# A macaron block on one Trainium2 core: the first FFN's last product as seven half products, transposed back for the mixer

## The chip, the cores and the metric

The kernel runs on one core of a Trainium2 chip. The core has five engines that run side by side and meet through semaphores: TensorE (PE, matrix products into PSUM; PEld is its loading of the stationary operand), VectorE (DVE), ScalarE (ACT), GpSimd (POOL) and SyncE (SP, which here only issues DMAs). The metric is the device time of one execution in microseconds (us). Three executions of the kernel before took 1169.32, 1170.34 and 1170.53 us; the median is 1170.34.

## The reference, cut to what matters

One layer, 512 tokens of 1024 channels, all float32; the inner width of an FFN is 2816.

```python
x = x + 0.5 * swiglu(rms_norm(x, ffn1_norm), ffn1_w1, ffn1_w3, ffn1_w2)   # (silu(h@w1) * (h@w3)) @ w2
h = rms_norm(x, mix_norm)
p = h @ w_in                               # 1024 x 5384: RWKV-7 columns, FoX columns, gates
...                                        # RWKV-7 recurrence, forgetting attention, gates
x = x + (gate_a * y_a + gate_b * y_b) @ w_out
x = x + 0.5 * swiglu(rms_norm(x, ffn2_norm), ffn2_w1, ffn2_w3, ffn2_w2)
out = rms_norm(x, final_norm)
```

## The kernel before

The program works through five stages in turn: the first FFN (FFN1), the mixer's input products with its preparation, the recurrence and the attention, the mixer's output products, and the second FFN (FFN2). Channels lie on the 128 partitions and the 512 tokens along the free axis, so `x` is kept as eight tiles `xT[c]` of 128 x 512.

**Products.** To keep float32 accuracy each operand is split into a high part (rounded to the format in which TensorE takes 512 columns in one pass) and a low remainder, and a product of a 128 x 128 weight block with 128 x 512 data is three matmuls: high*high, high*low, low*high (`mm3`, lines 122 to 124). For a block of eight weight tiles ACT makes the high part `whi` (L114) and DVE the low part `wlo` (L115). `whi` and `wlo` have two buffers each, the loaded `raw` tiles three.

**FFN1 and FFN2 up to the hidden values.** `ffn` (L453) runs over 22 blocks `j` of the hidden width. For each, `pa` and `pb` collect 8 x 3 matmuls, then `hidden` scales them with the token's `rstd`, applies SiLU and multiplies.

**The last product of FFN1** takes the hidden values as they are. `hidden` splits each block into `hh{j}` and `hl{j}`. For each of the eight channel tiles `m`, `pd` collects 22 x 3 matmuls with w2 blocks that are loaded in three pieces of 8, 8 and 6; DVE adds half of it to `xT[m]` (L518), and `mix_add(m)` saves the tile to DRAM through POOL's queue (L525), makes the mixer's operands `xh`, `xl` from it, and squares it for the norm.

**The last product of FFN2** uses `Seven` (L1147): both the hidden width and the output channels (and the tokens) are cut in halves, and a Strassen-like scheme forms the 2 x 2 block product from seven half-size products, with sums and differences of the blocks as operands. The sums of the weight blocks are made by DMA: a load through POOL's queue with `accum_op=add` adds the next block onto a tile `sum[g]` already in SBUF (L1195), and plain loads go through SP (L1197). Each of the seven products has 11 steps `k` and two halves `i` of 128 tokens, three matmuls each: 66 matmuls of 128 x 512. Its six weight tiles ("slots", two steps each) lie in tiles that earlier work has left: slot 0 in two `raw` tiles, slots 1 and 2 in `xh`, `xl` tiles, slots 3 and 4 in `whi`/`wlo`, slot 5 in the third `raw` tile. Here the data is the stationary operand and the weights are the moving one, so a result has tokens on the partitions and is added to a tile `O` of tokens x channels. That suits the kernel's output, which is stored so.

**The seam between FFN1 and the mixer.** The mixer's first two units are `psa` (72 columns of w_in) and `psg` (96 columns), both named `pl`, in the two banks of the PSUM pool `pm`. Behind `psa` two matmuls `ssum` add up the squares over the channels; ACT makes `rstd` from them (`finish`, with a load of the logarithm's table, L127); four transposes `rct` turn `rstd` to tokens on partitions (`rc`). DVE multiplies each unit by `rstd` (`u`, L583). From `psa` come `codes`, which the eight products `pz` need; these stand inside the two units `pk` that follow.

**What sets the order.** The program is written as one stream; the framework's planner puts each engine's instructions into an order of its own by a model of their times, within the data's dependences and with hints (`tc.issue_after`). On the chip each engine and each DMA queue takes its instructions strictly in that order, so an instruction that waits holds those behind it.

## Time and profile before

| | us |
|---|---|
| median of three runs | 1170.34 (1169.32 to 1170.53) |
| the profiled execution's own time | 1169.42 |
| its span, from the first to the last instruction | 1167.6 |
| TensorE busy in the span | 1150.1 (98%) |
| VectorE busy | 691.4 (59%) |
| ScalarE busy | 497.1 (43%) |
| GpSimd busy | 110.2 (9%) |
| mean DMA rate | 112 GB/s |

All starts below are counted from the span's start. A row of the timeline has start, length, engine, line, operation, the tile that it writes and those that it reads. Matmuls overlap in the pipeline, so the time that one adds to a stream is the distance between starts, not its own length. In a row of the windows the numbers behind the stretch are its length and then the busy time of PE, PEld, DVE, ACT and POOL, each with its count, the granted TensorE clock (1.00 is full), the DMA engines' share and their GB/s.

### The profile page before, as it was taken

What the parts mean: (1) busy time and instruction counts of PE and PEld (TensorE: products, weight loads), DVE (VectorE), ACT (ScalarE), POOL (GpSimd) and SP (SyncE); (2) the same over time, 40 slices, a digit from 0 to 9 for tenths busy, and PEclk for the clock granted to TensorE, in tenths of its full rate; (3) what the DMA queues carried; (4) which work ended last, traced back from release to release, by engine and by line L of the source; (5) the groups of instructions that cost most, each with busy time, mean ns of one, the idle gap of its engine ahead of it and who ended that gap; (6) DMA issues with size and microseconds to landing.
All of it is one profiled execution on the core that took longest, in us unless ns stands there. A gap on an engine that the chain in (4) does not pass through costs nothing.

```text
span 1167.6 us, 15706 instructions
## 1 busy us (share of the span) xinstructions
PE 1150.1 (98%) x6190; PEld 933.5 (80%) x6190; DVE 691.4 (59%) x996; ACT 497.1 (43%) x790; POOL 110.2 (9%) x159
## 2 busy tenths in 40 slices
PE   9999999999999999999999999899999999999997
PEld 7888888888887888887777786678888888888886
DVE  6645545543444598776776765677343446367874
ACT  6322222222223755345877665533332223236654
POOL 1200000001111111321000011112000000003210
PEclk9999999999999999999999999999999999999999
DMA  6333333333333333345112235543333333329981
GB/s 181 113 108 91 91 109 90 92 98 117 117 112 102 97 107 111 113 139 136 37 37 90 82 103 158 181 126 109 109 108 90 93 105 91 98 66 182 234 196 73
DMA packets 197865, 131.19 MB, mean 112 GB/s; under 512 B 10238, under 2 KB 180286, under 8 KB 197790
## 3 DMA queue, kind: packets, MB, share of 16 engines
q1 hardware_dynamic: 185198, 104.74, 30.6%
q0 software_dynamic: 9776, 23.60, 8.8%
q10 hardware_dynamic: 2816, 1.84, 0.5%
q8 instruction: 49, 0.80, 0.3%
q14 instruction: 26, 0.21, 0.1%
HBM read 119.47 MB, written 10.68 MB: 111 GB/s over the span
## 4 chain that ended last, share of the span: by engine, by line
PE 93%; ACT 2%; DVE 2%; DMA 2%; issue 1%; SPq 0%; ACTq 0%; DVEq 0%
PE pb L124 7%; PE pb L122 7%; PE pb L123 7%; PE pa L124 7%; PE pa L122 7%; PE pa L123 7%; PE pd L123 3%; PE pd L124 3%; PE pd L122 3%; PE pgt L122 3%; PE pgt L124 2%; PE pgt L123 2%; PE pk L123 2%; PE pk L122 2%; PE pk L124 2%; PE X L124 1%
## 5 line engine op out<-in xcount | busy, mean ns | idle before, releaser
L114 ACT CAST whi<-raw 128x1024 fp32r<-128x1024 f32 (+2 forms) x174 | 173.6, 999 | 510.7 <-PE pa L123 158.4
L115 DVE TENSOR_TENSOR wlo<-raw,whi 128x1024 fp32r<-128x1024 f32 (+2 forms) x174 | 202.2, 1162 | 86.7 <-ACT whi L114 86.7
L124 PE MATMUL pb<-xh,wlo 128*128 128x512 f32 x344 | 134.8, 392 | 0.1
L123 PE MATMUL pb<-xl,whi 128*128 128x512 f32 x344 | 134.1, 390 | 0.0
L124 PE MATMUL pa<-xh,wlo 128*128 128x512 f32 x344 | 134.1, 390 | 0.0
L122 PE MATMUL pb<-xh,whi 128*128 128x512 f32 x344 | 134.0, 390 | 0.0
L122 PE MATMUL pa<-xh,whi 128*128 128x512 f32 x344 | 134.0, 389 | 0.0
L123 PE MATMUL pa<-xl,whi 128*128 128x512 f32 x344 | 134.0, 389 | 0.0
L466 DVE TENSOR_TENSOR fb<-pb,rstd 128x512 f32<-128x512 f32 x43 | 29.7, 691 | 132.3 <-PE pb L124 132.3
L462 DVE TENSOR_TENSOR fa<-pa,rstd 128x512 f32<-128x512 f32 x43 | 29.7, 691 | 82.1 <-PE pa L124 82.1
L124 PEld LDWEIGHTS pb<-xh,wlo 128*128 128x128 f32 x344 | 64.6, 188 | 13.7 <-DVE wlo L247 0.6
L123 PEld LDWEIGHTS pb<-xl,whi 128*128 128x128 f32 x344 | 64.6, 188 | 13.6
L123 PEld LDWEIGHTS pa<-xl,whi 128*128 128x128 f32 x344 | 64.6, 188 | 13.5
L124 PEld LDWEIGHTS pa<-xh,wlo 128*128 128x128 f32 x344 | 64.6, 188 | 13.4
L122 PEld LDWEIGHTS pa<-xh,whi 128*128 128x128 f32 x344 | 64.6, 188 | 13.3
L122 PEld LDWEIGHTS pb<-xh,whi 128*128 128x128 f32 x344 | 64.6, 188 | 13.1
L122 PE MATMUL pd<-hh,whi 128*128 128x512 f32 x176 | 68.5, 389 | 0.0
L123 PE MATMUL pd<-hl,whi 128*128 128x512 f32 x176 | 68.5, 389 | 0.0
L124 PE MATMUL pd<-hh,wlo 128*128 128x512 f32 x176 | 68.5, 389 | 0.0
L122 PE MATMUL pgt<-xh,whi 128*128 128x512 f32 x128 | 53.7, 419 | 0.0
L123 PE MATMUL pgt<-xl,whi 128*128 128x512 f32 x128 | 50.4, 393 | 0.0
L124 PE MATMUL pgt<-xh,wlo 128*128 128x512 f32 x128 | 50.2, 392 | 0.0
(482 smaller groups left out, 2231.9 us busy)
## 6 DMA issues: line engine op xcount, KB each, us to landing
raw<-in_ffn_w_dram SPq DMA_DIRECT2D x102, 512.0 KB
raw<-in_w_in_dram SPq DMA_DIRECT2D x40, 512.0 KB
raw<-in_w_out_dram SPq DMA_DIRECT2D x8, 512.0 KB
xS<-in_ffn_w_dram POOLq DMA_DIRECT2D x8, 512.0 KB, 8.1
raw<-in_ffn_w_dram SPq DMA_DIRECT2D x8, 384.0 KB
xS<-in_ffn_w_dram SPq DMA_DIRECT2D x6, 512.0 KB
gsave<-gs SPq DMA_DIRECT2D x9, 256.0 KB
xin<-in_x_dram SPq DMA_DIRECT2D x8, 256.0 KB
```

Source lines behind the costliest of these rows:

```text
L114: (hi_eng or act).copy(hi[:], raw[:])
L115: (eng or dve).tensor_tensor(lo[:], raw[:], hi[:].bitcast(F32), op=ALU.subtract)
L122: pe.matmul(ps, whi, xhi, start=first, stop=False, skip_group_check=onto)
L123: pe.matmul(ps, whi, xlo, start=False, stop=False, skip_group_check=onto)
L124: return pe.matmul(ps, wlo, xhi, start=False, stop=last, skip_group_check=onto)
L462: dve.tensor_tensor(a[:], pa[:], nrm.rstd[:], op=ALU.mult)
L466: dve.tensor_tensor(b[:], pb[:], nrm.rstd[:], op=ALU.mult)
```

## The change

FFN1's last product is done by `Seven` as well. The class moves ahead of FFN1 and gets two children: `Last` for FFN2 (as before), `Middle` for FFN1. `Middle` adds onto a tile `O1` of tokens x channels, into which x is loaded a second time during the hidden blocks, with the first weight sums. During the seventh product each 128 x 128 block of `O1` is turned back by a transpose on TensorE (`turn`, L672): channel tiles 4 to 7 first, copied to `xT` by ACT, saved, and scaled to `xh`, `xl`; of tiles 0 to 3 the token blocks 2 and 3 at once, 0 and 1 behind the last matmuls, all in four PSUM banks (`low`) from which the mixer's operands are made directly. The units `psa` and `psg` take channel tiles 4 to 7 first, then 0 to 3. The norm's sums of squares now come from `O1` (ACT, with an accumulating output, four per half of the channels); `root` makes `rc` from them on 128 x 4 values, and `spread_root` brings it to all partitions with one float32 matmul (`rows`) against four diagonal tiles `dg`. `ssum`, `rct`, the squares of `xT` and POOL's additions of them are gone at this place. Tiles 0 to 3 are copied to `xT` and saved later (`keep`). The two first `pk` units get banks of the pool `pf`.

In both FFNs the seventh product now takes its steps in the order 0, 1, 6 to 10 for both halves, then 2 to 5 for one half after the other (before: 0 to 5, then 6 to 10), the sixth product's two results are added in the other order, and two weight splits are placed a little earlier.

```diff
+    KH, TH, LO, HI = KF // 2, T // 2, slice(0, D // 2), slice(D // 2, D)
+    class Seven:
...
+        def load(s, n, g):
+            r, c, more = ((0, 0, 0), (0, 1, 1), (1, 1, 1), (1, 0, 1), (1, 1, 0), (0, 1, 1), (1, 0, 0))[n]
...
+            if more:
+                nc.gpsimd.dma_start(s.sum[g], src, accum_op=ALU.add)
+            else:
+                with tc.issue_after(loads[-1].ins):
+                    nc.sync.dma_start(s.sum[g], src)
...
+            for n in range(6):
+                for g in range(6):
+                    put(n, min(2 * g + (5 if n == 0 else 3), 11 if n == 5 else 99), s.weight, n + 1, g)
...
+            first_k, last_k = (0, 1, 6, 7, 8, 9, 10), (2, 3, 4, 5)
+            for k in first_k:
+                for i in range(2):
+                    s.mm = mm(V, 6, i, k, True)
+                for f, *a in after.get((6, k), ()):
+                    f(*a)
+                s.between(k)
+            for i in range(2):
+                for k in last_k:
+                    s.mm = mm(V, 6, i, k, True)
+                    s.ending(i, k)
+                s.out(V[i][:], i, LO, 0.5)
+                s.finished(i)
...
-    def mix_add(c):
-        nc.gpsimd.dma_start(xsave[c], xT[c][:])
-        mix.add(c)
-
-    ffn(nrm, ffn1_w1, ffn1_w3, ffn1_w2, mix_add, {2: load_params, 4: masks, 10: place_params}, (first, second))
+    class Middle(Seven):
+        def turn(s, c, bs, ps=None, behind=None):
+            if ps is None:
+                ps = bank("xt", pm)
+            with tc.issue_after(behind.ins):
+                for b in bs:
+                    s.turned = pe.transpose(ps[:, b * P:(b + 1) * P], s.O[:, b, c * P:(c + 1) * P], ident[:])
+            return ps
...
+        def between(s, k):
+            if k == 7:
+                s.low = [bank(f"xt{c}", q_) for c, q_ in enumerate((pf, pf, pr, pr))]
+            c = {7: 4, 8: 5, 9: 6, 10: 7}.get(k)
+            if c:
+                ps = s.turn(c, range(NB), behind=s.mm)
+                act.copy(xT[c][:], ps[:])
+                nc.gpsimd.dma_start(xsave[c], xT[c][:])
+                mix.scale(c)
+                s.turn(c - 4, (2, 3), s.low[c - 4], s.mm)
+
+        def ending(s, i, k):
+            if i == 1 and k == 3:
+                for c in range(4):
+                    s.turn(c, (0,), s.low[c], s.mm)
...
+    def tail(s, behind):
+        for c in range(4):
+            s.turn(c, (1,), s.low[c], behind)
+        for c in range(4):
+            s.parts = mix.scale(c, act, s.low[c][:])
+        with tc.issue_after(s.parts[0].ins):
+            s.power(1, LO, sums[0])
+
+    def root(rc):
+        dve.tensor_tensor(rc, sums[0][:], sums[1][:], op=ALU.add)
+        act.activation(rc, rc, AF.Ln, bias=epsr[:, 0:1], scale=1.0 / D)
+        act.activation(rc, rc, AF.Exp, scale=-0.5)
+        dg = tmp("dg")
+        for b in range(NB):
+            dve.tensor_scalar(dg[:, b * P:(b + 1) * P], ident[:], rc[:, b:b + 1], None, op0=ALU.mult)
+        return dg
+
+    def spread_root(dg, behind):
+        ps = bank("rows", pr)
+        with tc.issue_after(behind.ins):
+            pe.matmul(ps[:], ones, dg[:], start=True, stop=True)
+        mix.rstd = xp.tile([P, T], F32, tag="rstd", name="rstd")
+        dve.tensor_copy(mix.rstd[:], ps[:])
+
+    def keep(s):
+        for c in range(4):
+            act.copy(xT[c][:], s.low[c][:])
+            nc.gpsimd.dma_start(xsave[c], xT[c][:])
...
+    ffn(nrm, ffn1_w1, ffn1_w3, ffn1_w2, make1, {2: load_params, 4: masks, 10: place_params}, (first, second),
+        {5 + 2 * j: (lambda j=j: beside1(j)) for j in range(8)})
...
-        mms = mix.cols(psa[0:72, :], *load_w([(0, W[:, COL_W:COL_W + 64]), (64, W[:, COL_F:COL_F + 8])], KD, 72), 72)
-        mix.parts()
-        summed = mix.finish(mms[-1])
...
+        mms = mix.cols(psa[0:72, :], *wa, 72, [seven1.turned] * 2, ks=(4, 5), end=False)
+        tail(seven1, mms[-1])
+        mms = mix.cols(psa[0:72, :], *wa, 72, [seven1.turned] * 2, ks=(6, 7), begin=False, end=False)
+        mms = mix.cols(psg[0:96, :], *wg, 96, [mms[-1]] * 4, ks=range(4, KD), end=False)
+        mms = mix.cols(psa[0:72, :], *wa, 72, [mms[-1]] * 4, ks=range(4), begin=False)
+        mms = mix.cols(psg[0:96, :], *wg, 96, [mms[-1]] * 4, ks=range(4), begin=False)
+        with tc.issue_after(seven1.parts[0].ins), tc.issue_after(seven1.parts[1].ins):
+            diag = root(rc[:])
+        spread_root(diag, mms[1])
         tc.keep_in_program_order(act.preload_act_table_set("sigmoid_and_others"))
-        mix.cols(psg[0:96, :], *load_w(win(COL_G, 96), KD, 96), 96, [summed])
...
+        keep(seven1)
+        o1.close()
...
-            ps = bank("pk")
+            ps = bank("pk", pf)
```

In the order of TensorE's instructions, this stood at the seam from FFN1 to the mixer: the last six matmuls of `pd` and the first six of the unit `psa`, whose tile is named `pl`.

```order
L122 MATMUL pd<-hh_1884,whi 128x512
L123 MATMUL pd<-hl_1885,whi 128x512
L124 MATMUL pd<-hh_1884,wlo 128x512
L122 MATMUL pd<-hh_1958,whi 128x512
L123 MATMUL pd<-hl_1959,whi 128x512
L124 MATMUL pd<-hh_1958,wlo 128x512
L122 MATMUL pl<-xh_2049,whi 72x512
L123 MATMUL pl<-xl_2050,whi 72x512
L124 MATMUL pl<-xh_2049,wlo 72x512
L122 MATMUL pl<-xh_2049,whi 72x512
L123 MATMUL pl<-xl_2050,whi 72x512
L124 MATMUL pl<-xh_2049,wlo 72x512
```

Now TensorE has there, behind the last three matmuls of the seventh product (`V` is its PSUM tile), transposes into the four banks `xt` of tiles 0 to 3 and, between two groups of them, the first six matmuls of `psa`, on channel tiles 4 and 5.

```order
L123 MATMUL V_1933<-sxl_1894,q_354 128x512
L124 MATMUL V_1933<-sxh_1893,q_354 128x512
L672 MATMUL xt_2521<-ident,O_339 128x128
L672 MATMUL xt_2522<-ident,O_339 128x128
L672 MATMUL xt_2523<-ident,O_339 128x128
L672 MATMUL xt_2524<-ident,O_339 128x128
L122 MATMUL pl<-xh_2532,whi 72x512
L123 MATMUL pl<-xl_2533,whi 72x512
L124 MATMUL pl<-xh_2532,wlo 72x512
L122 MATMUL pl<-xh_2532,whi 72x512
L123 MATMUL pl<-xl_2533,whi 72x512
L124 MATMUL pl<-xh_2532,wlo 72x512
```

Four more transposes stand behind these rows, then 18 matmuls on tiles 4 to 7, 24 on tiles 0 to 3, `rows`, and the first `pk` unit; from the second `pk` unit on, the order of TensorE is that of before, but for the places of single `pz` and `pn` matmuls.

ScalarE's rows at the same place, before: the last squares and the norm, with two table loads and the cast `whi` for the first `pk` unit between them.

```order
L187 ACTIVATE sq<-xT_115 128x512
L202 CAST shi<-acc 128x512
L127 ACT_TABLE_LOAD
L114 CAST whi<-raw 128x1024
L129 ACTIVATE rln<-ssum,epsr 128x512
L213 ACTIVATE rstd<-rln 128x512
L570 ACT_TABLE_LOAD
L561 ACTIVATE la<-u,omu 64x512
```

Now: the operands of tiles 0 to 3, the last square, the four copies of `keep`, `root`, a table load, and only then the casts for the two `pk` units.

```order
L175 ACTIVATE xh_2685<-xt_2523,par 128x512
L175 ACTIVATE xh_2685<-xt_2524,par 128x512
L592 ACTIVATE osq,ss_341<-O_339 128x512
L729 COPY xT_108<-xt_2521 128x512
L729 COPY xT_108<-xt_2522 128x512
L729 COPY xT_109<-xt_2523 128x512
L729 COPY xT_109<-xt_2524 128x512
L713 ACTIVATE rc<-rc,epsr 128x4
L714 ACTIVATE rc<-rc 128x4
L803 ACT_TABLE_LOAD
L114 CAST whi<-raw 128x1024 x2
L785 ACTIVATE la<-u,omu 64x512
```

The copies have moved ahead of `root` and of the casts on ScalarE's queue, and the logarithm's table load has gone from here to the start of the seven products.

A little earlier on ScalarE, where there were only casts of w2 and squares before, the casts of the weights of `psa` (128x576) and `psg` (128x768) now stand among the copies of tiles 4 to 7.

```order
L592 ACTIVATE osq,ss_342<-O_339 128x512 x2
L592 ACTIVATE osq,ss_341<-O_339 128x512 x2
L114 CAST whi<-raw 128x576
L689 COPY xT_110<-xt 128x512 x2
L114 CAST whi<-raw 128x768
L689 COPY xT_111<-xt 128x512 x2
L592 ACTIVATE osq,ss_341<-O_339 128x512
```

So the copy of tile 4 waits for the load of the weights of `psa`, which SP issues behind the seventh product's six sums and behind the release of slot 0.

## The prediction

> **What bounds the kernel now.** I read the page's busy times first, then the chain that ended last, then one table of windows by stage.

> ```profile
> PE 1150.1 (98%) x6190; PEld 933.5 (80%) x6190; DVE 691.4 (59%) x996; ACT 497.1 (43%) x790; POOL 110.2 (9%) x159
> PE 93%; ACT 2%; DVE 2%; DMA 2%; issue 1%; SPq 0%; ACTq 0%; DVEq 0%
> 250.50:376.50 126.00, 126.00 (x557) 103.11 (x556) 51.69 (x59) 30.46 (x36) 16.32 (x15) 1.00 0.38 113
> 1045.00:1160.40 115.40, 115.30 (x509) 95.20 (x507) 83.45 (x94) 64.03 (x83) 26.33 (x23) 1.00 0.76 169
> 376.50:400.00 23.50, 23.50 (x106) 18.67 (x105) 12.38 (x16) 17.18 (x24) 0.00 (x0) 1.00 0.35 98
> 400.00:540.00 140.00, 140.00 (x831) 114.35 (x830) 114.47 (x184) 69.85 (x99) 29.82 (x56) 1.00 0.39 113
> 540.00:710.00 170.00, 165.30 (x1644) 127.45 (x1642) 113.99 (x244) 123.50 (x305) 10.08 (x18) 0.99 0.30 86
> ```

> TensorE is busy 98% of the span and 93% of the last chain. The windows say where that is strict: in FFN1's last product (250.5 to 376.5), at the seam (376.5 to 400) and up to 540 us it never idles, and the clock is full. Time on TensorE there is time on the path. The second window is the model for what FFN1 gets: FFN2's seven products, where TensorE idles 0.1 us in 115.4 although DVE's load rises from 51.69 of 126 us to 83.45 of 115.4 and the DMA share from 0.38 to 0.76. Only the recurrence (540 to 710) has 4.7 us without a matmul.

> **The change part by part.** First what a matmul adds to a stream: the first and the last of 24 consecutive ones in FFN2's sixth product. Then the nearest rows to what is new or goes: four transposes inside a stream, float32 matmuls of 128x512 (`yc`) inside one, and the two groups at the seam that disappear.

> ```profile
> 1139.73 0.39 PE L122 MATMUL X<-swhi,q 128*128 128x512 f32 x1
> ...
> 1144.95 0.39 PE L124 MATMUL X<-sraw,q 128*128 128x512 f32 x1
> 828.73 0.39 PE L123 MATMUL pb<-xl,whi 128*128 128x512 f32 x1
> 828.97 0.60 PE L1142 MATMUL ot<-ident,xS 128*128 128x128 f32 x4
> 829.32 0.48 PE L124 MATMUL pb<-xh,wlo 128*128 128x512 f32 x1
> 829.63 0.40 PE L122 MATMUL pb<-xh,whi 128*128 128x512 f32 x1
> 707.50 0.39 PE L122 MATMUL ppj<-yh,whi 128*128 128x512 f32 x1
> 707.73 2.74 PE L1062 MATMUL yc<-V,center 128*128 128x512 f32 x6
> 709.90 0.79 PE L123 MATMUL ppj<-yl,whi 128*128 128x512 f32 x1
> L209 PE MATMUL ssum<-shi,onesr x3: 392/393/395, 27.1 to 817.1; 128*128 128x512 f32 x3
> L575 PE MATMUL rct<-ident,rstd x4: 270/272/273, 382.5 to 382.8; 128*128 128x128 f32 x4
> ```

> The pitch is (1144.95 - 1139.73) / 23 = 0.227 us. Around the four transposes, from the end of the matmul before (828.73 + 0.39 = 829.12) to the end of the second behind (829.63 + 0.40 = 830.03), pass 0.91 us; less two pitches that is 0.456, or 0.114 each. The six `yc` take 710.69 - 707.89 - 0.227 = 2.57 us, 0.43 each.

> - *The product.* Before: 8 tiles x 22 steps x 3 = 528 matmuls. Now: 7 products x 11 x 2 x 3 = 462 of the same shape. 66 fewer x 0.227 = **-14.98 us**, all on the path.
> - *Transposes.* 32 new ones, 32 x 0.114 = **+3.65**. They stand in groups of one to four, and I have a row for four only; at worst a lone one takes a whole pitch, 32 x 0.227 = 7.3. No row shows it cheaper, so 3.65 is also the floor. I take it, since most stand in groups.
> - *Norm.* Two `ssum` (ordinary matmuls by length) go: **-0.45**. Four `rct` go: **-0.46**. One float32 `rows` comes: **+0.43**.
> - *Hidden in FFN1's blocks:* SP issues four loads of `O1` and six first sums among the `raw` loads, and DVE's split per block becomes splits of four blocks at once. Cost nothing: SP's loads run ahead, TensorE never idled beside the same loads in FFN2. If that cover is gone, a `raw` tile comes late and both `pa` and `pb` wait for it.
> - *Hidden in the seven products:* 24 accumulating loads on POOL's queue, 42 weight splits and 21 operand splits on ACT and DVE. The cover is the 104.8 us of matmuls, which must outlast each chain from a load to its slot. The tightest one in FFN2 is slot 4 of the second product:

> ```profile
> 1074.99 1.05 ACT L140 CAST swhi<-sxh 128x1024 fp32r<-128x1024 f32 x1 [4.76 <-DMA sxh<-in_ffn_w_dram]
> 1076.07 1.23 DVE L141 TENSOR_TENSOR swlo<-sxh,swhi 128x1024 fp32r<-128x1024 f32 x1 [2.44 <-ACT swhi L140]
> 1081.25 0.39 PE L122 MATMUL Y<-swhi,q 128*128 128x512 f32 x1
> xS<-in_ffn_w_dram POOLq DMA_DIRECT2D x8, 512.0 KB, 8.1
> third<-in_ffn_w_dram POOLq DMA_DIRECT2D x4, 512.0 KB, 9.8
> ```

> ACT waited for the load, but `swlo` was ready at 1077.30 and its step began at 1081.25: a margin of 3.95 us beside loads that land in 8.1 to 9.8. FFN1 issues the same loads in the same order, with one DVE instruction more (1.2 us, the rest of group 1, which FFN2 does earlier) at the start of the products. The margin covers it: cost 0.

> - *The seam.* Here is what FFN2 does not show. The nearest rows for each step of the new chain:

> ```profile
> 354.13 0.99 SPq L107 DMA_DIRECT2D raw<-in_w_in_dram x2
> xsave<-xT POOLq DMA_DIRECT2D x8, 256.0 KB, 2.3
> 1160.33 0.69 DVE L1229 SCALAR_TENSOR_TENSOR O<-V,O 128x512 f32<-128x512 f32 x1 [0.60 <-PE V L124]
> L247 ACT ACTIVATE xh<-xtp,par x1: 687/687/687, 6.4 to 6.4; 128x512 fp32r<-128x512 f32 x1
> L247 DVE SCALAR_TENSOR_TENSOR xl<-xtp,par,xh x2: 751/751/751, 5.9 to 7.1; 128x512 fp32r<-128x512 f32 x2
> L247 ACT COPY xT<-xtp x8: 567/587/588, 8.6 to 17.7; 128x512 f32<-128x512 f32 x8
> 1161.06 0.63 ACT L1233 ACTIVATE osq<-O 128x512 f32<-128x512 f32 x1 [1.36 <-DVE O L1229]
> 1161.59 0.19 ACT L1233 ACTIVATION_READ_ACCUMULATOR osq<-O 128x1 f32 x1
> 1161.81 0.29 ACT L1244 ACTIVATE fr<-ss,cb 128x1 f32<-128x1 f32 x1
> 1162.14 0.20 ACT L1245 ACTIVATE fr<-fr 128x1 f32<-128x1 f32 x1
> 374.45 1.28 ACT L127 ACT_TABLE_LOAD   x1
> 376.45 1.05 ACT L114 CAST whi<-raw 128x1024 fp32r<-128x1024 f32 x1 [0.71 <-issue]
> 377.53 1.23 DVE L115 TENSOR_TENSOR wlo<-raw,whi 128x1024 fp32r<-128x1024 f32 x1 [2.37 <-ACT whi L114]
> ```

> I lay them on a clock that starts with the seventh product. TensorE: 42 matmuls to 9.5, 24 transposes 2.7 more, 24 matmuls to 17.7, then 4 transposes, 6 matmuls, 4 transposes to 20.0, 18 matmuls on tiles 4 to 7 to 24.0, 12 and 12 on tiles 0 to 3 to 29.5, `rows` to 29.9, `pk`.

> *Operands of tiles 0 to 3.* From 20.2 four `xh` of 0.69 run to 23.0; the first `xl` is there at 21.6, the last at 23.8. TensorE needs the first at 24.0: hidden by the 18 matmuls, with 2.4 us in hand. Without them TensorE would stand about 1.6 us.

> *Casts for `pk`.* Behind these, ACT has a square (0.63 + 0.19), four copies (4 x 0.59), two small ones (0.49), the table load (1.28): 27.9. Cast to 29.0, `wlo` to 30.2. TensorE's third `pk` matmul, the first that reads `wlo`, stands at 29.9 + 0.45 = 30.35. That leaves 0.15 us. The six handovers between engines in this chain cost 0.03 to 0.04 each in these rows (1161.02 to 1161.06, 377.50 to 377.53), so it comes about 0.1 late; the 0.71 of idle that the cast's row shows behind a table load would make it 0.8. A gain is excluded, since TensorE had no idle here before. I take **+0.3**.

> *Weights of `psa`.* Slot 0 is free after 12 matmuls (2.9); two issues (0.99) give 3.9. Landing is between 2.3 (a save of 256 KB) and 9.8 us: 6.2 to 13.7. ACT casts (at most 1.05) and copies tile 4 (0.59): 7.8 to 15.3. TensorE needs that bank again for tile 6 after 41 matmuls and 15 transposes, at 11.0. So 0 to +4.3; I take 0, because at this place no POOL load is in flight any more and a plain load of the same size is nearest to the 2.3.

> - *FFN2's tail.* 12 instead of 15 matmuls stand behind the first half's end, so DVE's idle of 0.60 us before the last `O<-V` shrinks by 0.68: **+0.1**, at most the whole 0.68.

> Sum: -14.98 + 3.65 - 0.45 - 0.46 + 0.43 + 0.3 + 0.1 = **-11.4 us**. The profiled execution took 1169.42, so its like would take 1158.0; it lies 0.9 under the median of the runs, and 1170.34 - 11.4 = **1158.9**.

> **The rivals.** *A: the seam stalls.* The first `pk` unit or tile 6's transposes wait as above. For it: ACT takes its instructions in order, so a load holds four copies. Against it: SP issues early. Price 0.8 + 4.3 = 5.1 at the most instead of the 0.3, so up to 1163.7; half of it gives 1161.2.

> *B: the norm arrives late and VectorE drags.* `rstd` comes at 29.9 + 0.35 + 0.69, 1.0 us behind the start of the first `pk`. Before, it came well ahead:

> ```profile
> 378.11 0.63 ACT L213 ACTIVATE rstd<-rln 128x512 f32<-128x512 f32 x1
> 382.81 0.48 PE L122 MATMUL pk<-xh,whi 128*128 128x512 f32 x1
> ```

> 382.81 - 378.74 = 4.1 ahead. DVE and ACT thus start the mixer 5.1 us later against TensorE. Against it: DVE idles 11.1 of 23.5 us here before, and the `pz` products, the first to need it, come two `pk` units later, at 29.9 + 48 x 0.227 = 40.8; by the rows' lengths `codes` are done near 38.8. If the idle were under 5 us, up to 5.1 would come back: 1164.0.

> *C, slower: the accumulating loads come late in FFN1.* Four of the six later products use them. A landing longer than 9.8 + 3.95 stalls TensorE in each. To eat 11.4 us and pass the bound below, each must stall 3.4 us, which is a landing of 17.2 us; at twice the 9.8 the time is 1158.9 + 4 x 5.85 = 1182.3. For it: the DMA share of 0.76. Against it: FFN2 has the same loads, and TensorE idles 0.1 us there.

> *D: POOL's issues are held by DVE.* If each issue had to sit out four subtractions of 1.23 us, 4.9 us, the margin would be passed by 1.0 us in four products: 1162.9. The row that bears on it:

> ```profile
> L1195 POOL DMA_DIRECT2D xS<-in_ffn_w_dram x7 | 8.7, 1236 | 25.7 <-DVE sraw L141 15.7 <-DVE sxl L141 10.0
> ```

> Seven issues take 1236 ns each while DVE is busy 72% of the window, and none is stretched. [...]

> **How the numbers follow.** The three runs spread over 1.2 us, so 0.2%, 2.3 us, is about what a measurement can tell from no change. Chances: the forecast 0.66, A 0.17, B 0.05, D 0.04, C 0.06, and 0.02 for a sum of small losses that ends within 0.2%. So faster 0.92, the same 0.02, slower 0.06. The predicted time is 1158.9. Low: the sum without the 0.4 at seam and tail, less the 1.0 by which the fastest run lies under the median, 1157.4. High: lone transposes' 3.65 and half of A's most, 2.6, on top: 1165.2. C lies outside.

> **What would show it.** In the changed profile: FFN1's products as one window without TensorE idle, `xt` 32 times, the pitch still 0.227 there. Wrong would be a wait of TensorE for `whi` or `wlo` at `pk` (A), of `xt` for a copy (A), of `pz` for `codes` (B), of `swlo` for a load in the seven products (C, D), or a granted clock under 1.00. The prediction fails if the mixer, starting some 11 us sooner, does not also end so much sooner.

## The result: faster, and by more than forecast

The changed kernel takes 1156.11 us (median of 4 runs, 1154.99 to 1156.81) against 1169.83 us (1169.15 to 1170.53) for the kernel before in the same comparison: ratio 0.9882, 95% interval 0.9865 to 0.9899. That is 13.7 us or 1.2% less, where 11.4 were forecast; 1156.1 lies 1.3 us under the lower end of the range. The profiled execution took 1155.48 us with a span of 1153.6, so against the profile of before the span is 14.0 us shorter.

First the page of the changed kernel, engines and then the last chain by engine:

```profile
PE 1137.7 (99%) x6152; PEld 922.9 (80%) x6152; DVE 719.7 (62%) x1010; ACT 538.2 (47%) x848; POOL 127.1 (11%) x177
PE 88%; DVE 4%; ACT 3%; issue 3%; DMA 2%; POOL 0%; SPq 0%; ACTq 0%; POOLq 0%; DVEq 0%
```

TensorE is busy 12.4 us less and 99% of the span. The windows by stage (stretch, length, then busy time of PE, PEld, DVE, ACT and POOL, granted clock, DMA share, GB/s): the last hidden blocks with FFN1's first six products (the first of their matmuls starts at 240.72), the seventh and the seam up to `rows`, the two `pk` units and what follows, the place of the mixer's first wait, and, in two rows, the rest up to the recurrence's end.

```profile
234.00:340.90 106.90, 106.90 (x473) 88.51 (x472) 78.58 (x80) 58.91 (x65) 27.91 (x24) 1.00 0.80 173
340.90:371.10 30.20, 30.20 (x149) 23.04 (x148) 16.60 (x32) 15.84 (x32) 4.49 (x9) 1.00 0.50 145
371.10:400.00 28.90, 28.90 (x127) 23.63 (x126) 20.14 (x25) 22.07 (x33) 4.24 (x12) 1.00 0.35 98
400.00:420.00 20.00, 19.12 (x111) 15.34 (x110) 19.49 (x28) 13.11 (x19) 1.13 (x3) 1.00 0.42 119
420.00:540.00 120.00, 120.00 (x733) 97.57 (x734) 89.45 (x152) 52.61 (x75) 26.63 (x44) 1.00 0.43 121
540.00:700.00 160.00, 155.53 (x1586) 119.44 (x1585) 110.66 (x240) 118.90 (x299) 8.08 (x15) 0.99 0.28 82
```

TensorE does not idle from the first of the seven products to 400 us, with the DMA share up to 0.80 and the clock at 1.00. It loses 0.88 us at one place between 400 and 420.

To find where 14.0 us come from, I set the start of the same matmul in both profiles side by side, from front to back:

| the same instruction | before | after | difference |
| --- | --- | --- | --- |
| second matmul of the first `pk` unit | 383.13 | 371.75 | -11.38 |
| `pk` matmul that reads the late `wlo` | 413.02 | 402.73 | -10.29 |
| last `ppj` step ahead of `rwkv_proj` | 730.01 | 719.46 | -10.55 |
| first `ppj` matmul behind the late load | 753.67 | 741.84 | -11.83 |
| eleventh matmul behind it | 757.84 | 744.53 | -13.31 |
| VectorE's last step, the last output | 1162.38 | 1149.09 | -13.29 |
| end of the span | 1167.6 | 1153.6 | -14.0 |

Down to the seam it is the forecast. In the mixer's input products 1.1 us are lost again. Then, between the mixer's output products, far from anything that the prediction looked at, 2.8 us more are won between 730 and 758 us, and 0.7 at the very end.

The place of the 2.8, before: POOL's issues of `fg` and of most of the `xS` loads, two of SP's rows, then TensorE.

```profile
739.27 0.54 POOL L1134 DMA_DIRECT2D fg<-in_final_norm_dram  x1 [23.58 <-PE ppj L124]
739.81 3.77 POOL L1110 DMA_DIRECT2D xS<-xsave  x7
740.46 0.46 SPq L1197 DMA_DIRECT2D third<-in_ffn_w_dram  x1
741.19 13.54 SPq L107 DMA_DIRECT2D raw<-in_rwkv_proj_dram  x4
753.67 0.50 PE L122 MATMUL ppj<-ya,whi 128*128 128x512 f32 x1 [2.91 <-ACT whi L114]
754.98 0.63 PE L122 MATMUL ppj<-ya,whi 128*128 128x512 f32 x1
755.41 0.63 PE L123 MATMUL ppj<-ya,whi 128*128 128x512 f32 x1
```

The chain of waits there (start, length), and the windows around it, one during the burst of transfers and one behind the wait:

```profile
741.19 11.71 DMA raw<-in_rwkv_proj_dram
```

```profile
747.00:749.00 2.00, 2.00 (x10) 1.66 (x9) 1.71 (x4) 1.15 (x2) 0.00 (x0) 1.00 1.05 391
753.67:757.67 4.00, 4.00 (x10) 2.89 (x11) 3.09 (x5) 2.76 (x5) 0.00 (x0) 0.57 0.26 72
```

After, the same views without the window in the burst (`third` now stands far from it):

```profile
852.09 0.58 SPq L556 DMA_DIRECT2D third<-in_ffn_w_dram  x1
741.84 0.50 PE L122 MATMUL ppj<-ya,whi 128*128 128x512 f32 x1 [1.61 <-ACT whi L114]
743.15 0.40 PE L123 MATMUL ppj<-ya,whi 128*128 128x512 f32 x1
743.38 0.39 PE L124 MATMUL ppj<-ya,wlo 128*128 128x512 f32 x1
```

```profile
730.64 10.44 DMA raw<-in_rwkv_proj_dram
```

```profile
741.84:745.84 4.00, 4.00 (x16) 3.03 (x17) 3.73 (x7) 3.01 (x6) 0.00 (x0) 1.00 0.22 67
```

A weight load of 256 KB for `rwkv_proj` shares the DMA engines, which are full meanwhile (share 1.05 at 747 to 749 us), with eight loads of `xS` (256 KB each) and `fg` (512 KB), which POOL issues in a row, and in the kernel before with `third`, the third of FFN2's first sums, which SP issues 0.7 us ahead of it. In the changed kernel `third` goes out at 852. At the burst's 391 GB/s its 512 KB take 1.34 us; the weight load lands after 10.44 us in place of 11.71, 1.27 less, and TensorE waits 1.61 in place of 2.91, 1.30 less. Behind the longer wait the granted clock was 0.57 over 4 us, and matmuls followed each other at 0.43 us (754.98, 755.41) in place of 0.23 (743.15, 743.38): that is the other 1.5.

`third` moved because of two lines of the diff. `load` in `Seven` now issues the plain first sums under `with tc.issue_after(loads[-1].ins)`, and FFN2 uses the same class; its `Last` is not "as before" in this respect. The two lines also hold back a second of FFN2's first sums (`sum`, issued at 769.95 before and at 874.82 now). It stood behind this place, and from 758 us to VectorE's last step the difference stays at 13.3 us.

### The profile page after: what moved, and what is told of

It reads as the page before. It is cut to its first block, busy times and chain, and to the rows that moved or that the text cites. A ratio compares the mean times of both kernels' runs of the same rounds, so it can differ in the third digit from the quotient of the medians.

```text
span 1153.6 us, 15781 instructions
## 1 busy us (share of the span) xinstructions
PE 1137.7 (99%) x6152; PEld 922.9 (80%) x6152; DVE 719.7 (62%) x1010; ACT 538.2 (47%) x848; POOL 127.1 (11%) x177
## 4 chain that ended last, share of the span: by engine, by line
PE 88%; DVE 4%; ACT 3%; issue 3%; DMA 2%; POOL 0%; SPq 0%; ACTq 0%; POOLq 0%; DVEq 0%
PE pb L124 7%; PE pb L122 7%; PE pb L123 7%; PE pa L124 7%; PE pa L122 7%; PE pa L123 7%; PE pgt L122 3%; PE X L124 3%; PE X L123 3%; PE X L122 3%; PE pgt L124 2%; PE pgt L123 2%; PE Y L124 2%; PE Y L123 2%; PE Y L122 2%
## 5 line engine op out<-in xcount | busy, mean ns | idle before, releaser
L114 ACT CAST whi<-raw 128x1024 fp32r<-128x1024 f32 (+1 forms) x150 | 150.0, 1002 | 396.8 <-PE pa L123 138.7
L115 DVE TENSOR_TENSOR wlo<-raw,whi 128x1024 fp32r<-128x1024 f32 (+1 forms) x150 | 174.8, 1166 | 38.6 <-ACT whi L114 38.3
L124 PE MATMUL pb<-xh,wlo 128*128 128x512 f32 x344 | 134.7, 392 | 0.1
L123 PE MATMUL pb<-xl,whi 128*128 128x512 f32 x344 | 134.0, 389 | 0.0
L124 PE MATMUL pa<-xh,wlo 128*128 128x512 f32 x344 | 133.9, 389 | 0.0
L122 PE MATMUL pb<-xh,whi 128*128 128x512 f32 x344 | 133.9, 389 | 0.0
L123 PE MATMUL pa<-xl,whi 128*128 128x512 f32 x344 | 133.8, 389 | 0.0
L122 PE MATMUL pa<-xh,whi 128*128 128x512 f32 x344 | 133.8, 389 | 0.0
L124 PEld LDWEIGHTS pb<-xh,wlo 128*128 128x128 f32 x344 | 64.7, 188 | 13.7 <-DVE wlo L251 0.6
L123 PEld LDWEIGHTS pb<-xl,whi 128*128 128x128 f32 x344 | 64.6, 188 | 13.6
L122 PEld LDWEIGHTS pa<-xh,whi 128*128 128x128 f32 x344 | 64.6, 188 | 13.4
L124 PEld LDWEIGHTS pa<-xh,wlo 128*128 128x128 f32 x344 | 64.5, 188 | 13.5
L123 PEld LDWEIGHTS pa<-xl,whi 128*128 128x128 f32 x344 | 64.6, 188 | 13.4
L122 PEld LDWEIGHTS pb<-xh,whi 128*128 128x128 f32 x344 | 64.6, 188 | 13.0
L122 PE MATMUL pgt<-xh,whi 128*128 128x512 f32 x128 | 53.7, 419 | 0.0
L123 PE MATMUL pgt<-xl,whi 128*128 128x512 f32 x128 | 50.3, 393 | 0.0
L124 PE MATMUL pgt<-xh,wlo 128*128 128x512 f32 x128 | 50.2, 392 | 0.0
L553 POOL DMA_DIRECT2D xT<-in_ffn_w_dram x12 | 14.7, 1229 | 228.8 <-DVE sraw L141 219.1
L553 POOL DMA_DIRECT2D xS<-in_ffn_w_dram x8 | 10.0, 1252 | 258.9 <-issue 233.3
L124 PE MATMUL pk<-xh,wlo 128*128 128x512 f32 x96 | 37.6, 391 | 0.9 <-DVE wlo L115 0.9
## 6 DMA issues: line engine op xcount, KB each, us to landing
raw<-in_ffn_w_dram SPq DMA_DIRECT2D x86, 512.0 KB
raw<-in_w_in_dram SPq DMA_DIRECT2D x40, 512.0 KB
xT<-in_ffn_w_dram POOLq DMA_DIRECT2D x12, 512.0 KB, 8.8
xT<-in_ffn_w_dram SPq DMA_DIRECT2D x9, 512.0 KB
sxl<-in_ffn_w_dram POOLq DMA_DIRECT2D x8, 512.0 KB, 8.3
sxh<-in_ffn_w_dram POOLq DMA_DIRECT2D x8, 512.0 KB, 8.6
raw<-in_w_out_dram SPq DMA_DIRECT2D x8, 512.0 KB
xS<-in_ffn_w_dram POOLq DMA_DIRECT2D x8, 512.0 KB, 8.6
```

Of the source, the lines that this page charges most:

```text
L114: (hi_eng or act).copy(hi[:], raw[:])
L115: (eng or dve).tensor_tensor(lo[:], raw[:], hi[:].bitcast(F32), op=ALU.subtract)
L122: pe.matmul(ps, whi, xhi, start=first, stop=False, skip_group_check=onto)
L123: pe.matmul(ps, whi, xlo, start=False, stop=False, skip_group_check=onto)
L124: return pe.matmul(ps, wlo, xhi, start=False, stop=last, skip_group_check=onto)
L553: nc.gpsimd.dma_start(s.sum[g], src, accum_op=ALU.add)
```

## The experiments

**The changed kernel again, and `third` put back into the burst.** The first is the measure for the others. The experiments ran on three chips; the median of the kernel before lay between 1168.89 and 1169.23 us in each comparison, so their times are set side by side here.

> The changed kernel again, nothing edited, as the measure for the others on this chip. Theory A (the extra 2.8 us come from FFN2's first sum `third`, which the change moved out of a burst of transfers between the mixer's output products): 13.7 us under the kernel before, and in the profile again a wait of TensorE of about 1.6 us at a `ppj` step of `rwkv_proj`, with the granted clock at 1.00 behind it. Rival B (how long that wait is, and whether the clock falls behind it, is chance from one execution to the next): the wait is as likely near 2.9 us with the clock near half speed for some 3 us behind it.

Measured: 1155.28 us (1155.19 to 1156.32), ratio to the kernel before 0.9882 (0.9869 to 0.9895). The wait is 1.47 us, the load lands after 10.29 us, the clock behind it is 1.00. As theory A has it.

```
     class Seven:
-
+        held = True
...
             else:
-                with tc.issue_after(loads[-1].ins):
+                with tc.issue_after(loads[-1].ins) if s.held else ExitStack():
                     nc.sync.dma_start(s.sum[g], src)
...
     class Last(Seven):
+        held = False
```

> The changed kernel, but FFN2's first sums are no longer held behind the last weight load, so that `third` (512 KB) goes out among the loads of `rwkv_proj` as it did before the change. No other engine's order changes. Theory A: TensorE waits 2.9 us there in place of 1.6, the matmuls behind the wait run at about 0.43 us each for some 3 us, and the kernel is 2.5 to 3 us slower than the changed one (about 11 us under the kernel before, which is what my sum gave). Rival B: no difference beyond 0.5 us.

Measured: 1157.65 us, ratio 0.9899 (0.9885 to 0.9913); 2.4 us slower than the changed kernel and 11.5 under the kernel before. The two intervals overlap (0.9885 to 0.9895), but each of the four runs (1156.38 to 1158.47) is slower than each of the changed kernel's on the same chip. Only SP's order differs from the changed kernel's, in `third` and `sum`. The load, the wait and the clock behind it (chain, timeline, windows):

```profile
730.39 11.64 DMA raw<-in_rwkv_proj_dram
```

```profile
729.66 0.46 SPq L556 DMA_DIRECT2D third<-in_ffn_w_dram  x1
742.80 0.50 PE L122 MATMUL ppj<-ya,whi 128*128 128x512 f32 x1 [2.86 <-ACT whi L114]
```

```profile
742.80:746.80 4.00, 4.00 (x16) 3.00 (x17) 3.71 (x7) 3.00 (x6) 0.00 (x0) 1.00 0.25 70
```

The load and the wait are as long as before the change. The clock, though, did not fall in this execution, which was the fastest of its four (1156.38; the others up to 1158.47). So the wait belongs to `third`, while behind a wait of 2.9 us the clock fell in one profiled execution (the kernel before, 0.57) and not in another (this one, 1.00); that much of rival B is true.

**The kernel before with this part of the change alone.**

```
             else:
-                nc.sync.dma_start(s.sum[g], src)
+                with tc.issue_after(loads[-1].ins):
+                    nc.sync.dma_start(s.sum[g], src)
```

> The kernel before, with only this part of the change: FFN2's first sums held behind the last weight load. Theory A: 2.5 to 3 us faster than the kernel before, the wait at `ppj` about 1.6 us, the clock at 1.00 behind it. Rival B: no difference. Rival C (the extra gain needs the mixer's earlier start, or comes from FFN2's new step order): no difference either, and then e1 shows none.

Measured: 1166.16 us against 1169.11, ratio 0.9975 (0.9965 to 0.9985): 2.95 us faster, with none of the seven products in FFN1. Eight runs lie within 1165.88 to 1166.67, where the twenty runs of the kernel before on this chip go from 1167.22 to 1171.70. Timeline and windows:

```profile
751.98 0.50 PE L122 MATMUL ppj<-ya,whi 128*128 128x512 f32 x1 [1.74 <-ACT whi L114]
```

```profile
751.98:755.98 4.00, 4.00 (x16) 3.02 (x17) 3.73 (x7) 3.00 (x6) 0.00 (x0) 1.00 0.23 68
```

From both sides the two lines are worth 2.4 to 3.0 us. Rival C, that the extra gain needs the earlier mixer or FFN2's new steps, is out.

**More in the burst, and less.** To the kernel with `third` put back, one more load of 512 KB:

```
     third = fp.tile([P, 2, T], F32, name="third")
+    nc.sync.dma_start(O[:, 0], x[0, 0:P, :])
```

> The kernel of the run that let `third` go out early again, with one more load of 512 KB (of `x`, into the tile `O`, which is overwritten later) ahead of `third` in the same burst. Theory A, transfers sharing the engines: the weight load lands 1.3 us later again (13 us), TensorE waits about 4.2 us, and this wait is long enough for the clock to fall in every execution: 1.3 us for the wait and up to 1.6 for the clock, so 1.5 to 3 us slower than that run (1157.65). If the load's time doesn't go by the bytes beside it, nothing changes.

Measured: 1161.06 us, ratio 0.9931 (0.9919 to 0.9944), 3.4 us slower than with `third` alone and 0.4 more than expected at most, in runs that lie within 1160.17 to 1161.28. Its chain, timeline and windows at the place:

```profile
732.41 12.83 DMA raw<-in_rwkv_proj_dram
```

```profile
746.01 0.61 PE L122 MATMUL ppj<-ya,whi 128*128 128x512 f32 x1 [4.32 <-ACT whi L114]
```

```profile
746.01:750.01 4.00, 4.00 (x10) 2.94 (x11) 3.08 (x5) 2.66 (x5) 0.00 (x0) 0.57 0.24 69
```

Another 512 KB, another 1.2 us on the load and 1.5 on the wait, and the clock fell to 0.57. Not all of the distance between these two executions (4.7 us) belongs to the burst: TensorE's last matmul ahead of the wait already ends 1.75 us later (741.69 against 739.94), lost in the recurrence, where a stretch of half clock came at another moment (558.5 in place of 553.9). The wait adds 1.46, and some 1.3 come behind it. Now the other way, `xS` and `fg` behind the loads of `w_out`:

```
-        for c in range(KD):
-            nc.gpsimd.dma_start(xT[c][:], xsave[c])
...
             wh, wl = load_w([(0, w_out[0][:, m * P:(m + 1) * P])], KD, P)
+            with tc.issue_after(loads[-1].ins):
+                nc.sync.dma_start(xT[m][:], xsave[m])
...
-    nc.gpsimd.dma_start(fg[:], final_norm.unsqueeze(0).broadcast_to([P, D]))
+    with tc.issue_after(loads[-1].ins):
+        nc.sync.dma_start(fg[:], final_norm.unsqueeze(0).broadcast_to([P, D]))
```

> The changed kernel, with the other loads of the burst moved too: the eight `xS` loads (256 KB each) and `fg` (512 KB), which POOL issues together while the loads of `rwkv_proj` run, go out on SP one behind each weight load of `w_out`. Theory A (TensorE waits there because the weight load shares the DMA engines with 2.5 MB that nobody needs yet): the wait of 1.5 us at `ppj` goes, and the kernel is 1.5 us faster than the changed one, 15.3 us under the kernel before. If the weight load is late for its own sake (issued too late by its free buffer), the wait stays and the time is the same; a new wait of `pw` on an `xS` tile would make it slower.

Measured: 1153.64 us, ratio 0.9872 (0.9857 to 0.9886), 1.6 us under the changed kernel's 1155.28 as expected; the intervals overlap, but each of the four runs (1153.36 to 1154.67) is faster than each of the changed kernel's. TensorE's window over the stage, here:

```profile
728.00:745.00 17.00, 16.92 (x74) 13.35 (x73) 13.18 (x22) 8.57 (x16) 0.00 (x0) 1.00 0.32 89
```

and in the changed kernel:

```profile
728.00:745.00 17.00, 15.30 (x64) 11.35 (x64) 11.26 (x18) 7.59 (x15) 4.78 (x9) 1.00 0.72 231
```

The wait is gone (TensorE idles 0.08 us of these 17 in place of 1.70), the DMA share falls from 0.72 to 0.32. The weight load was late because of what shared the engines with it, not because it was issued late.

**What lowers the clock.** The kernel before, with matmuls whose result is overwritten in front of the unit that waits; nine, then twelve.

```
+        filled = []
...
             ps = bank("ppj")
+            if wt is rwkv_proj and m == 4:
+                with tc.issue_after(filled[-1].ins):
+                    for _ in range(9):
+                        pe.matmul(ps[:], onesr[:], y[0][0], start=True, stop=True)
...
```

> The kernel before, with nine more matmuls (their result is overwritten) in front of the `ppj` unit that waits for the late load: TensorE idles about 0.8 us in place of 2.9, and the load comes no sooner. If the clock falls because TensorE stood still for 2.9 us, the slow matmuls behind it go and the kernel is about 1.6 us faster, although it does more work. If the slow matmuls have another cause (the operands, the burst of transfers), the time stays the same within 0.3 us, or is up to 2 us longer if the nine don't fit into the wait.

> The kernel before with twelve overwritten matmuls (2.7 us) in place of nine in front of the late load, which with nine still left 2.1 us of idle time and slow matmuls behind it in the profiled execution. If standing still is what lowers the clock, the idle time left (0.2 us where the load takes 11.7 us, 1.5 us where it takes 13) is no longer than the waits of 1.5 to 1.7 us behind which the clock stayed at 1.00 in six profiles: the granted clock is 1.00 behind the wait, the executions lie closer together than those of the kernel before (1167.2 to 1171.7), and their median is 1 to 1.6 us under its own. If the burst or the late load itself lowers the clock, nothing changes, or the time grows by what doesn't fit.

Measured: 1168.23 us (ratio 0.9992, 0.9983 to 1.0002) with nine and 1168.87 (0.9994, 0.9985 to 1.0003) with twelve: no difference that can be told, neither the gain of 1 to 1.6 us nor a loss, and with twelve the executions hardly lie closer together (1167.11 to 1170.37) than those of the kernel before beside them (1167.14 to 1171.37). In both profiled executions the load took 13.0 us in place of 11.7, for a reason that no run shows, so that the idle time shrank less than the matmuls filled: 2.14 us were left with nine and 1.41 with twelve. With 2.14 the clock behind it was 0.63 (in the slowest of the twelve executions, 1171.71), with 1.41 it was 1.00. The times do not settle the question. What the profiles show is this list of idle times at this place and the clock over the 4 us behind them; the middle row is explained below:

| idle, us | 1.41 to 1.74 (eight profiles) | 2.14 | 2.86 | 2.91 | 4.32 |
| --- | --- | --- | --- | --- | --- |
| most of it in one piece of 3.41 us | at most 1.66 | 2.14 | 1.67 | 2.82 | 3.17 |
| granted clock | 1.00 in each | 0.63 | 1.00 | 0.57 | 0.57 |

```profile
750.85:754.26 3.41, 0.59 (x2) 0.30 (x2) 0.61 (x2) 1.26 (x3) 0.00 (x0) 1.00 0.83 222
754.26:757.67 3.41, 3.41 (x9) 2.60 (x9) 2.50 (x5) 2.17 (x4) 0.00 (x0) 0.50 0.29 82
```

With nine matmuls in front, 2.14 us idle:

```profile
753.56:756.97 3.41, 1.27 (x4) 0.60 (x4) 1.07 (x2) 1.72 (x4) 0.00 (x0) 1.00 0.26 63
756.97:760.38 3.41, 3.41 (x9) 2.65 (x8) 2.71 (x5) 1.61 (x3) 0.00 (x0) 0.50 0.30 88
```

With `third` put back, 2.86 us idle:

```profile
738.20:741.61 3.41, 1.74 (x8) 1.13 (x6) 1.02 (x2) 0.00 (x0) 0.00 (x0) 1.00 1.07 343
741.61:745.02 3.41, 2.22 (x8) 1.53 (x9) 2.24 (x4) 2.18 (x4) 0.00 (x0) 1.00 0.40 101
```

The wait of 2.14 us lies whole in one piece; the wait of 2.86 is cut by a border into 1.67 and 1.19. Read so, the order is right: at this place the clock stayed where TensorE idled up to 1.67 us of a piece, and fell in the next piece where it idled 2.14 or more. All twelve profiles that have the wait fit this, but no run moved a border on purpose. It is not a full rule either: in the recurrence the clock fell behind a piece with 1.61 us of idle time in the kernel before (559.70 to 563.11) and behind one with 1.54 in the changed kernel (550.69 to 554.10), where it stayed behind one with 1.60 at the wait (738.42 to 741.83). As an estimate from these numbers for this place, a wait of 2.9 us leaves the clock at 1.00 when a border cuts it into two parts below a limit between 1.67 and 2.14. If the border is as likely at one point as at another, which no run shows, 0.4 to 1.4 of every 3.41 us do so, and the clock falls in 60 to 87% of the executions.

**Does the seam's time reach the end?** Each of the 32 transposes twice:

```
-                for b in bs:
+                for b in [b for b in bs for _ in range(2)]:
                     s.turned = pe.transpose(ps[:, b * P:(b + 1) * P], s.O[:, b, c * P:(c + 1) * P], ident[:])
```

> The changed kernel with each of its 32 transposes done twice. My step 'transposes' had 0.114 us each and all of it on the path: 3.7 us slower than the changed kernel, about 10.1 us under the kernel before, and the whole 3.7 us still there at the end. If part of TensorE's time at the seam is covered (the mixer waits for VectorE or the weights anyway), it costs less than 3 us, and the sum was right by luck only.

Measured: 1158.79 us, ratio 0.9916 (0.9901 to 0.9931): 3.5 us over the changed kernel, a little under the 3.7 expected. In the profile the second matmul of the first `pk` unit is 3.15 us later (374.90 against 371.75), 0.10 for each added transpose, and VectorE's last step 3.17 later (1152.26 against 1149.09). TensorE's time at the seam goes one to one to the end.

**FFN2's steps in their old order.**

```
     class Last(Seven):
+        first_k, last_k = range(6), range(6, 11)
...
```

> The changed kernel with FFN2's seventh product in its order of before: steps 0 to 5 for both halves and 6 to 10 per half, so that 15 in place of 12 matmuls stand behind the first half's end. My step 'FFN2's tail' says 0.1 us faster than the changed kernel, at most 0.7. The rival, that the new order gives part of the extra gain (the span ends 4.5 us behind VectorE's last step in the changed kernel and 5.2 in the kernel before), says 0.7 us slower.

Measured: 1155.97 us, ratio 0.9891 (0.9876 to 0.9906). The median is 0.7 us above the changed kernel's, which is what the rival says, but the intervals overlap, and the profile speaks against it. There the first matmul behind the late load is already 0.9 us later (742.74 against 741.84), lost in the recurrence, where the stretch of half clock came at another moment (558.8 in place of 554.1). From that matmul to VectorE's last step (1149.95) pass 407.21 us, and 407.25 in the changed kernel. The span still ends 4.5 us behind that step (1154.5). So neither the 0.7 us at the end of the span nor anything else of the extra gain is seen to come from the order of steps.

**The norm later, and VectorE's order.** `rows` behind the first `pk` unit:

```
-        spread_root(diag, mms[1])
...
+        pk0 = bank("pk", pf)
+        ahead = mix.cols(pk0[:], *load_w(win(DA), KD, P), P)
+        spread_root(diag, ahead[-1])
```

> The changed kernel with `rows`, and so the norm, one `pk` unit (24 matmuls, 5.4 us) later. In the changed kernel the mixer showed one wait behind the seam, 0.9 us at a `pk` unit about 30 us on. If VectorE and ScalarE have room behind the seam, as my case against rival B had it, the planner moves the `pz` products a unit back and the time grows by less than 1 us. If rival B's mechanism binds as soon as they start later still, the wait grows with the delay, up to 5 us, and the kernel ends that much later.

Measured: 1155.71 us, ratio 0.9891 (0.9874 to 0.9907). `rows` starts 5.6 us later in the profile, and by the recurrence nothing of it is left (0.05 us at 492): VectorE has the room that the case against rival B claimed. The remaining wait, then, is a matter of order. TensorE's row in the changed kernel, and VectorE's ahead of it:

```profile
398.23 0.69 DVE L141 TENSOR_TENSOR klo<-ksq,khi 128x512 fp32r<-128x512 f32 x1
398.83 0.68 DVE L891 TENSOR_TENSOR gs<-pgt,rstd 128x512 f32<-128x512 f32 x1
399.43 1.38 DVE L946 TENSOR_TENSOR G<-spare,Tall 64x512 f32<-64x512 f32 x2
400.84 0.69 DVE L915 SCALAR_TENSOR_TENSOR spare<-kt,spare 128x512 f32<-128x512 f32 x1
401.45 1.22 DVE L115 TENSOR_TENSOR wlo<-raw,whi 128x1024 fp32r<-128x1024 f32 x1
402.73 0.50 PE L124 MATMUL pk<-xh,wlo 128*128 128x512 f32 x1 [0.88 <-DVE wlo L115]
```

In the kernel before, `spare` stood behind this `wlo`; now the planner has put it ahead.

```
+        lows.append((eng or dve).tensor_tensor(lo[:], raw[:], hi[:].bitcast(F32), op=ALU.subtract))
+        if len(lows) == 50:
+            for i in scaled[:3]:
+                tc.add_manual_dep(i.ins, lows[-1].ins.name, mybir.DependencyInfo(
+                    mybir.DependencyClass.NoSync, mybir.DependencyReason.DATA), reason="order")
...
+            scaled.append(dve.scalar_tensor_tensor(k[:], t[:], 1.0, k[:], op0=ALU.add, op1=ALU.mult))
...
+                scaled.append(dve.tensor_tensor(G[p][q][s, :, 1, :], ch(r)[s], Pp[s, :, 1:C + 1], op=ALU.mult))
```

> The changed kernel, with VectorE's order behind the seam changed at one place: the `wlo` for which a `pk` unit waits 0.9 us (near 402 us) goes ahead of the two products for `G` and the one for `spare` that stand before it. If that wait is a matter of VectorE's order (the mixer starts later against TensorE, so the order leaves less room), the wait goes and the recurrence starts up to 0.9 us sooner, at most 0.9 us faster than the changed kernel. If VectorE simply has too much to do there, another wait takes its place, and the time stays.

Measured: 1154.31 us, ratio 0.9871 (0.9856 to 0.9886). The wait is gone and the unit 0.82 us earlier; 0.56 of it are still there at the output products. The medians differ by 1.0 us, but their intervals overlap; that it is faster is likely, not shown. Nor is this one `wlo` all that moved: the planner answered the new dependence by rearranging other instructions behind it as well (some 170 of TensorE's 6152 stand elsewhere), so the run shows that the wait is a matter of order, not what this one place is worth.

**Both together.** The edits of the late loads and of this order in one kernel:

> The edits of the two runs that were faster than the changed kernel together: `xS` and `fg` behind the loads of `w_out`, and the one `wlo` behind the seam ahead of VectorE's four instructions. They touch different stages, so their gains add if the first is not given back in between: 1.6 (late loads) and 0.6 to 1.0 (order) give 2.2 to 2.6 us under the changed kernel, 1152.7 to 1153.1. If the start that the order gives the recurrence is lost again before the output products, only the 1.6 are left: 1153.7.

Measured: 1152.45 us (1151.42 to 1152.84), ratio to the kernel before 0.9856 (0.9838 to 0.9874): 2.8 us under the changed kernel, a little better than the 2.2 to 2.6 expected, and the fastest here. TensorE from the end of the recurrence through the output products:

```profile
690.00:760.00 70.00, 69.92 (x315) 53.09 (x314) 45.43 (x72) 36.08 (x61) 3.75 (x7) 1.00 0.47 146
```

## Why the prediction was right to the seam and short behind it

*Product, transposes.* Right. In the changed kernel four transposes stand in the stream ahead of the first `pl` matmul, and the fp32 `rows` ahead of the first `pk`:

```profile
358.22 0.39 PE L123 MATMUL V<-sxl,q 128*128 128x512 f32 x1
358.45 0.40 PE L124 MATMUL V<-sxh,q 128*128 128x512 f32 x1
358.69 0.60 PE L672 MATMUL xt<-ident,O 128*128 128x128 f32 x4
359.36 0.39 PE L123 MATMUL pl<-xl,whi 128*72 128x512 f32 x1
370.44 0.39 PE L124 MATMUL pl<-xh,wlo 128*96 128x512 f32 x1
370.67 1.02 PE L723 MATMUL rows<-dg,onesr 128*128 128x512 f32 x2
371.75 0.39 PE L123 MATMUL pk<-xl,whi 128*128 128x512 f32 x1
```

From 358.22 to 359.36 pass 1.14 us; less three pitches of 0.227 that is 0.46 for four, 0.115 each where 0.114 was taken. Lone ones were no dearer: over the seventh product, 340.91 to 358.45, 65 pitches and 24 transposes take 17.54 us, 0.116 each.

*Norm.* A term mis-sized. The step priced `rows` as one record of 0.43; the profile has it as two (x2), where each matmul of a product is one, and 370.44 to 371.75 less two pitches is 0.86. The six records of `yc` that gave the price were three matmuls (line 1062 issues one for each `p`): count records against the code before dividing.

*Hidden in FFN1's blocks and in the seven products.* Right for FFN1: 106.9 of 106.9 us busy. Rivals C and D are refuted by the same row; no product waited for a load, and of POOL's 24 accumulating issues there (L553) the longest took 1.36 us, against a median of 1.20. (The prediction's "none is stretched" is not quite so: of the eight `xS` issues before, one took 1.51 us against a median of 1.19.)

*The seam.* Operands hidden, as said. Weights of `psa`: 0, as taken; the cast waited for its load (347.28, 6.4 on the prediction's clock, at the near end of its 6.2 to 13.7), and the copy of tile 4 behind it on ScalarE's queue started at 347.86, although its transposes had ended at 346.96. Casts for `pk`: 0 in place of 0.3, since `wlo` was ready at 370.17 and its first reader stood at 371.98. Rival A is refuted. The prediction's sum to this point is -11.5. With 0.43 more for `rows` and 0.3 less for the casts it is the measured -11.38; that the forecast came so near here is in part luck, since the two errors hid each other.

*Rival B.* Refuted as priced (codes ready at 379.86, `pz` at 382.45), but the step behind it, that nothing changes once the seam is passed, was 1.1 us wrong: the planner put one instruction ahead of a `wlo`, and VectorE's lead no longer covered it.

*FFN2's tail.* 0 in place of 0.1 at VectorE's last step.

*The step that failed* is "Hidden in FFN1's blocks". It read the diff's edit of `load` as FFN1's matter (six first sums among the weight loads) and costed it at nothing. The class is shared, so the same two lines also took FFN2's `third` out of a burst between the mixer's output products. The prediction had not looked at that stage at all. The runs put 2.4 to 3.0 us on it, and without it the changed kernel takes 1157.65, 11.5 us under the kernel before, by the sum of the prediction. That this is the sum so exactly is luck in part, since neither the 1.1 us lost in the mixer nor the 0.7 won at the span's end was forecast. The chance of 0.92 for faster stands; the range was too narrow below, because its lower end only took out small losses and had no place for a gain outside the stages named. (Its terms give 1157.5, not 1157.4.)

Open: the span ends 4.5 to 4.7 us behind VectorE's last step in eight profiles (the changed kernel's two and six of its variants) and 5.1 to 5.3 in the other six (the kernel before, its three variants, and the two with late loads). In that time stand only this step's own 0.75 us, the issues of the last output's stores by ScalarE and SyncE (0.37 and 0.33), and the program's closing semaphores (1150.25 to 1153.57 in the changed kernel), and no run settles its 0.7 us.

## What to carry to other kernels

When a helper is shared, price its edit at every caller: here a new ordering hint took `third` from 740 to 852 us, and both stages needed a row. Look for weight loads that wait beside transfers nobody needs yet; the bytes that `third` adds to the burst, divided by the burst's rate, gave the longer wait to within 0.1 us, and moving 2.5 MB behind later loads gave 1.6 us. A longer wait can cost more than itself: at the place studied here the clock was halved for 3.41 us behind three of the four waits of 2.1 us and more, and behind none of the eight under 1.8. In a stream that TensorE bounds, count pitches and records: corrected for the records, the sum of some 11 us came out to within 0.1 at the seam, and time added there went one to one to the end.

## What the runs showed that I had not expected

A load of 512 KB that nobody waits for cost 2.4 to 3.0 us, twice the 1.34 that its bytes take at the burst's 391 GB/s: 1.3 for the wait, and up to 1.5 for matmuls at half clock behind it. A wait of 1.4 to 1.7 us left the clock alone in eight profiles, while behind one of 2.9 us it fell in one execution (2.82 of it in one piece of 3.41 us) and not in another (1.67 and 1.19 in two). This goes with times that scatter over 4.5 us (kernel before, twenty runs) in place of 0.8 (the same with `third` held, eight runs). And 5.6 us of delay to the norm cost nothing: the planner moved the products that need it a unit back.
